# Attention's TensorE order written out by hand: key tiles in pairs, kinds of matmuls grouped, the compressed branch a block ahead, fill tiles emitted last

## The chip, the cores and the metric

The kernel runs on one core of a Trainium2 chip. The metric is the device time of one execution in microseconds (us), the median over runs. TensorE multiplies matrices, VectorE, ScalarE and GpSimd (the profile's DVE, ACT and POOL) do the elementwise work, SyncE (SP) issues most of the DMAs. Each engine works off its own instructions in a fixed order and waits on semaphores for the others.

## The reference, cut to what matters

One block of a network for 1024 tokens of width 1024. A projection `x @ w_in` feeds three branches: `_nsa` (attention, A), `_spatial_gating` (B) and `_mlstm` (C). The outputs of the branches are gated, merged, projected, gated once more and normalized. What the change touches is branch A and the projections that share TensorE with it. Branch A has two groups of four heads; in each, a query sees compressed keys, selected blocks of keys and a window:

```python
p_cmp = _masked_softmax(s_cmp, d_cmp >= 0)                    # 63 compressed keys
o_cmp = einsum(p_cmp, v_cmp)
imp = einsum(p_cmp, overlap)                                  # importance of 16 blocks of 64 keys
top_score, top_idx = lax.top_k(score, 8)                      # 8 blocks for each query
...
o_sel = softmax(q k_sel - slopes * d, causal) v_sel           # the selected blocks
o_w   = softmax(q k_w - slopes * d, window of 256) v_w        # the window
o = gates[0] * o_cmp + gates[1] * o_sel + gates[2] * o_win
y_a = o * silu(a_z)                                           # a_z = x @ w
y_b = u * mixed * silu(b_z)                                   # u = gelu(b_u); b_u, b_z = x @ w
```

## The kernel before, in words

The kernel is written with Tile: the program is emitted in Python, and a planner orders each engine's instructions by priority (what is emitted earlier goes first, what is ready earlier may overtake), hands out the buffers of the pools and sets the semaphores. Each projection multiplies in three parts (high x high, low x high, high x low) to keep float32's accuracy, with operands split into `hi` and `lo`.

- `load_w` (lines 84 to 95) loads a weight tile of 128x1024 into `wraw`, casts it to `whi` on ScalarE (line 92) and subtracts for `wlo` on VectorE (line 93). Each of the three tags has two buffers, and every weight tile of attention and of the next stage goes through them.
- `proj_half` (line 129) makes one half of a projected tile: 24 matmuls of 512 columns into one bank of `pj`. A tile is two halves, 48 matmuls.
- `prep_group(g)` projects a group's k (one tile, lines 372 to 382) and q (two tiles, lines 390 to 403) into `KA`, `KB`, `QA`, `QB`.
- `attn_front(g, qb, d)` handles a block of 128 queries: the compressed branch (scores `ps_c` at line 427, softmax, for qb >= 4 the ranking of the blocks, transposes `ps_t`, `ps_co` at line 472, output `o`), the mask of the selected blocks (`ps_r` and line 464, into `QB[64:80]`), and then the row maxima of the window (`ps_w`) and the selected branch (`ps_s`), eight or twelve matmuls, each reduced by VectorE in `rowmax` (lines 409 and 412). The maxima are transposed (`ps_m`) and written into `QB[96:104]` at line 499.
- `attn_back(g, qb, d, st)` takes the key tiles of a block one after the other: two score matmuls into a bank of `ps_st` (lines 513, 514), the exponential on ScalarE into `pt` (line 516), on some tiles a mask on GpSimd, and four matmuls with the values into `ps_o` (line 536; eight instructions in the trace). The scores run one tile ahead (`AHEAD = 1`). At the end of the window and of the selected branch VectorE adds into `o` (lines 543 to 547), and `o` is transposed (`ps_ot`, line 551) into `ya`.
- `fill_az`, `fill_bu`, `fill_bz` project tiles of `a_z`, `b_u`, `b_z`, which nothing in attention waits for. Seven tiles are emitted in group 0's loop and five in group 1's, half a tile for each block and the rest behind the loop, so group 0's are emitted ahead of `prep_group(1)`.

For a group the loop emits `prep_group`, then for each block the front, half a fill tile and the back of the block before. The order on TensorE is the planner's. Behind attention follow `wtm` projections in 256 columns (line 150), the small work of branch B and the gates of branch C, and from 587 us Strassen products (line 792).

Of the kernel before, what the change touches and what calls it, by code (L numbers as in the profile page):

```python
# [26 lines left out]
WARM = 8  # L27
AHEAD = 1
WB = 2
# [16 lines left out]
def hybrid_kernel(ctx, tc, xm, pT, wfm, wvg, wtm, cmpw1, cmpw2, cpos, vecs, sgwT, sgb,  # L46
# [129 lines left out]

    def silu2(dst, src, n):

        t = tp.tile([P, 512], F32, tag="ge_a", bufs=2, name="si_a")
        act(t[:, :n], src, AF.Tanh, scale=0.5)  # L180
        stt(out=dst, in0=t[:, :n], scalar=1.0, in1=src, op0=OP.add, op1=OP.mult)
# [232 lines left out]

    def attn_front(g, qb, d):
        QA = d["QA"][qb // 2][:, qb % 2]
        QB = d["QB"][qb // 2][:, qb % 2]
        st = {}

        cb = pa2.tile([P, 4, 64], F32, tag="cb", bufs=1, name="cb")  # L420
# [18 lines left out]
        if qb >= 4:  # L439
# [19 lines left out]
            vv.tensor_scalar(out=rk, in0=rk, scalar1=7.5, scalar2=NEG, op0=OP.is_ge, op1=OP.mult)  # L459
            if "rk" in dbg:  # L460
                dump("rk", rk) if (g, qb) == (0, 5) else None
            pr = pst("m", 2, "ps_r")
            nc.tensor.transpose(pr[0:16, 0:P], rk, ident)
            vv.tensor_copy(QB[64:80, :, :], pr[0:16, 0:P].unsqueeze(1).to_broadcast([16, 4, P]))
        ptp = pst("m", 2, "ps_t")
        for a in range(2):
            nc.tensor.transpose(ptp[:, a * P:a * P + P], p[:, 2 * a:2 * a + 2, :], ident)
        pts = pa2.tile([P, 2, P], F32, tag="pts", bufs=2, name="pts")
        nc.any.tensor_copy(out=pts, in_=ptp[:, 0:256].rearrange("p (a q) -> p a q", a=2))
        pco = pst("m", 2, "ps_co")  # L470
        for a in range(2):
# [3 lines left out]
                      gates[:, qb, g * 4:g * 4 + 4].unsqueeze(2).to_broadcast([P, 4, 64]))  # L475
        st["o"] = o

        mx = pa2.tile([P, 8], F32, tag="mx", bufs=3, name="mx")
        mx2 = pa2.tile([P, 4], F32, tag="mx2", bufs=3, name="mx2")
        j0 = max(0, qb - 2)  # L480
        nw = (qb - j0 + 1) * P
        for h in range(HPG):
            pw = pst("m", 2, "ps_w")
            mm(pw[:, 0:nw], lhsT=QB[:, h, :], rhs=d["KBw"][:, j0 * P:j0 * P + nw], start=True, stop=True)
            rowmax(mx[:, 4 + h:5 + h], pw, nw, winm[:, 384 - nw:384] if qb >= 2 else zrow[:, 512 - nw:512])
        ns = (qb + 1) * P
        for h in range(HPG):
            for c0 in range(0, ns, 512):
                n = min(512, ns - c0)
                last = c0 + n == ns  # L490
# [3 lines left out]
                rowmax(dst[:, h:h + 1], pw, n, zrow[:, 512 - n:512] if last else None)  # L494
        if ns > 512:
# [4 lines left out]
                         in1=nblk.unsqueeze(2).to_broadcast([8, 4, P]), op=OP.mult)  # L500
        return st

    def attn_back(g, qb, d, st):
        QA = d["QA"][qb // 2][:, qb % 2].rearrange("p h q -> p (h q)")
        QB = d["QB"][qb // 2][:, qb % 2].rearrange("p h q -> p (h q)")
        o = st["o"]
        sc = pa2.tile([P, 16], F32, tag="osc", bufs=3, name="osc")
        tiles = [("w", j) for j in ([qb - 1, qb, qb - 2] if qb > 1 else range(qb + 1))] + [("s", j) for j in range(qb + 1)]

        def scores(br, j):  # L510
            sp = pst("st", 2, "ps_st")
            ks = slice(j * P, j * P + P)
            mm(sp, lhsT=d["KA" + br][:, ks], rhs=QA, start=True, stop=False)  # L513
            mm(sp, lhsT=d["KB" + br][:, ks], rhs=QB, start=False, stop=True)  # L514
            pt = pa2.tile([P, 4, P], F32, tag="pt", bufs=3, name="pt")
            act(pt.rearrange("p h q -> p (h q)"), sp, AF.Exp)  # L516
            if j == qb:
                nc.gpsimd.affine_select(out=pt, in_=pt, pattern=[[0, 4], [1, P]], compare_op=OP.is_ge,  # L518
                                        fill=0.0, base=0, channel_multiplier=-1)
            elif br == "w" and j == qb - 2:  # L520
                nc.gpsimd.affine_select(out=pt, in_=pt, pattern=[[0, 4], [-1, P]], compare_op=OP.is_gt,
                                        fill=0.0, base=0, channel_multiplier=1)
            return pt

        ahead = [scores(*t) for t in tiles[:AHEAD]]
        for i, (br, j) in enumerate(tiles):
            if i + AHEAD < len(tiles):
                ahead.append(scores(*tiles[i + AHEAD]))
            pt = ahead[i]
            first = i == 0 or tiles[i - 1][0] != br  # L530
            last = i == len(tiles) - 1 or tiles[i + 1][0] != br
            if first:
                po = pst("o", 2, "ps_o")
            vi = g if br == "s" else 2 + g
            for h in range(HPG):
                mm(po[:, h * 65:h * 65 + 65], lhsT=pt[:, h, :], rhs=V[:, j, vi, :],  # L536
                   start=(first and h == 0), stop=last, skip_group_check=True)
            if not last:
                continue
            po3 = po[:, 0:260].rearrange("p (h d) -> p h d", h=4)  # L540
            c0 = 0 if br == "w" else 8
            gi = (16 if br == "w" else 8) + g * 4
            vv.tensor_scalar_max(sc[:, c0:c0 + 4].unsqueeze(2), po3[:, :, 64:65], 1e-30)
            vv.reciprocal(sc[:, c0 + 4:c0 + 8], sc[:, c0:c0 + 4])
            vv.tensor_mul(sc[:, c0 + 4:c0 + 8], sc[:, c0 + 4:c0 + 8], gates[:, qb, gi:gi + 4])
            for h in range(HPG):
                stt(out=o[:, h, :], in0=po3[:, h, 0:64], scalar=sc[:, c0 + 4 + h:c0 + 5 + h], in1=o[:, h, :],
                    op0=OP.mult, op1=OP.add)
        pt2 = pst("o", 2, "ps_ot")
        for a in range(2):  # L550
            nc.tensor.transpose(pt2[:, a * P:a * P + P], o[:, 2 * a:2 * a + 2, :], ident)
        for a in range(2):
            y = ya[2 * g + a][:, qb * P:qb * P + P]
            if g == 0:
                nc.any.tensor_copy(out=y, in_=pt2[:, a * P:a * P + P])
            else:
                stt(out=y, in0=pt2[:, a * P:a * P + P], scalar=0.5, in1=y, op0=OP.mult, op1=OP.mult)

    yb = [yp.tile([P, T], F32, tag="y", bufs=YB, name="yb") for _ in range(4)]

    def fill_az(i):
        w = wf(FM["az"] + i)
        for half in range(2):
            po = pj()
            proj_half(po, w, half, xh, xl)
            y = ya[i][:, half * 512:half * 512 + 512]
            if i >= 2:
                silu2(y, po, 512)
            else:
                z = pa2.tile([P, 512], F32, tag="zz", bufs=1, name="zz")  # L570
                silu2(z, po, 512)
                stt(out=y, in0=z, scalar=0.5, in1=y, op0=OP.mult, op1=OP.mult)
            yield

    def fill_bu(i):
        w = wf(FM["bu"] + i)
        for half in range(2):
            po = pj()
            proj_half(po, w, half, xh, xl)
            gelu2(yb[i][:, half * 512:half * 512 + 512], po, 512)  # L580
            yield

    def fill_bz(i):
        w = wf(FM["bz"] + i)
        for half in range(2):
            po = pj()
            proj_half(po, w, half, xh, xl)
            z = pa2.tile([P, 512], F32, tag="zz", bufs=1, name="zz")
            silu2(z, po, 512)
            y = yb[i][:, half * 512:half * 512 + 512]  # L590
            vv.tensor_mul(y, y, z)
            yield

    for g in range(G):
        fills = chain(*([fill_az(2), fill_az(3), fill_bu(0), fill_bz(0), fill_bu(1), fill_bz(1), fill_bu(2)] if g == 0 else
                        [fill_az(0), fill_az(1), fill_bz(2), fill_bu(3), fill_bz(3)]))
        d = prep_group(g)
        prev = None
        for qb in range(NT):
            st = attn_front(g, qb, d)  # L600
            next(fills, None)
            if prev is not None:
                attn_back(g, prev[0], d, prev[1])
            prev = (qb, st)
        attn_back(g, prev[0], d, prev[1])
        for _ in fills:
            pass
    if "ya" in dbg:
# [637 lines left out]
```

## Time and profile before

| | us |
|---|---|
| median of 3 runs | 1365.41 (1363.35 to 1366.42) |
| the profiled execution | 1363.39 |
| its span, first to last instruction | 1361.6 |
| TensorE busy (PE) | 1334.0 |
| VectorE busy (DVE) | 849.0 |
| ScalarE busy (ACT) | 522.3 |

The times that the rows carry are counted from the span's start. Attention of group 0 runs from about 99 to 277 us, that of group 1 from about 323 to 495. A float32 matmul appears as two instructions of TensorE. Matmuls overlap, so that an instruction's own duration (0.39 us for 512 columns) is longer than the spacing of two (0.23); in the chain of work an instruction counts only until the next one starts. PEclk is the clock granted to TensorE as a share of 2.4 GHz.

### The profile page before, as it was taken

The numbers are of one execution on the slowest core, as the hardware profiler recorded it, in microseconds if no ns is written. First come the engines' busy times: TensorE is split into PE (matmuls) and PEld (weight loads), VectorE is DVE, ScalarE is ACT, GpSimd is POOL, SyncE is SP. The second block draws the span as 40 slices with busy tenths as digits, with TensorE's granted clock in tenths as the row PEclk, the third lists the DMA queues.
The fourth block names the chain that finished last, engine by engine and source line by source line (L and its number), as shares of the span: only waits on it lengthen the run. The fifth ranks groups of instructions, "written<-read, shape, count | busy, mean of one in ns | idle before, by whom it ended". The sixth has DMA issues, their size and how long they took to land.

```text
span 1361.6 us, 18953 instructions
## 1 busy us (share of the span) xinstructions
PE 1334.0 (98%) x7135; PEld 1127.7 (83%) x7135; DVE 849.0 (62%) x2006; ACT 522.3 (38%) x1040; POOL 158.4 (12%) x173
## 2 busy tenths in 40 slices
PE   8999999999999999999999999999999999999997
PEld 6977888887888998988888888888878887888786
DVE  6246777435777748657777678766444555334855
ACT  6353434344333343245455454554442212224211
POOL 0011212101221100001001010010000443000312
PEclk9999999999999999999999999999999999999998
DMA  9131011011110033433222232245346643114201
GB/s 318 32 71 47 24 28 47 19 52 55 55 55 20 17 110 93 141 93 124 97 83 99 94 124 93 62 135 190 117 166 212 201 140 108 47 62 136 96 32 47
DMA packets 48059, 127.46 MB, mean 94 GB/s; under 512 B 5208, under 2 KB 16344, under 8 KB 47968
## 3 DMA queue, kind: packets, MB, share of 16 engines
q1 hardware_dynamic: 47008, 123.11, 27.6%
q0 software_dynamic: 960, 3.15, 1.1%
q8 instruction: 56, 0.92, 0.3%
q14 instruction: 35, 0.29, 0.1%
HBM read 101.00 MB, written 25.23 MB: 93 GB/s over the span
## 4 chain that ended last, share of the span: by engine, by line
PE 85%; DVE 7%; DMA 3%; ACT 3%; issue 2%; POOL 0%; SPq 0%; ACTq 0%; DVEq 0%; POOLq 0%
PE ps_pj L129 19%; PE ps_a L792 13%; PE ps_b L129 9%; PE ps_b L792 7%; PE ps_o L536 7%; PE ps_g L1061 5%; PE ps_c L792 3%; PE ps_st L513 2%; PE ps_pj L150 2%; PE ps_v L138 2%; PE ps_st L514 2%; PE ps_e L1101 2%; PE ps_st L150 1%; PE ps_s L492 1%; DMA xraw<-in_xm_dram 1%
## 5 line engine op out<-in xcount | busy, mean ns | idle before, releaser
L536 PEld LDWEIGHTS ps_o<-V,pt 128*128 128x128 f32 x912 | 117.5, 191 | 12.2 <-ACT pt L516 3.3
L129 PE MATMUL ps_pj<-xh,whi 128*128 128x512 f32 x288 | 115.4, 401 | 2.4 <-DVE QA L402 2.4
L536 PE MATMUL ps_o<-V,pt 128*128 128x65 f32 x912 | 116.7, 269 | 0.5 <-POOL pt L518 0.3
L129 PE MATMUL ps_pj<-xh,wlo 128*128 128x512 f32 x288 | 114.6, 398 | 0.0
L129 PE MATMUL ps_pj<-xl,whi 128*128 128x512 f32 x288 | 114.3, 397 | 0.0
L516 ACT ACTIVATE pt<-ps_st 128x512 f32<-128x512 f32 x114 | 65.4, 594 | 103.7 <-PE ps_st L514 96.6
L792 PE MATMUL ps_a<-op_lo,sh 128*128 128x512 f32 x240 | 94.1, 392 | 0.0
L792 PE MATMUL ps_a<-op_hi,sh 128*128 128x512 f32 x240 | 93.8, 391 | 0.0
L792 PE MATMUL ps_a<-op_hi,sl 128*128 128x512 f32 x240 | 93.8, 391 | 0.0
L779 DVE TENSOR_TENSOR sl<-ss,sh 128x512 fp32r<-128x512 f32 x80 | 54.8, 688 | 59.1 <-ACT sh L778 58.9
L92 ACT CAST whi<-wraw 128x1024 fp32r<-128x1024 f32 x46 | 48.2, 1048 | 77.0 <-PE ps_b L129 46.8
L129 PE MATMUL ps_b<-sp_hi,wlo 128*128 128x512 f32 x192 | 74.8, 390 | 1.3 <-DVE wlo L93 1.3
L129 PE MATMUL ps_b<-sp_lo,whi 128*128 128x512 f32 x192 | 74.7, 389 | 0.0
L129 PE MATMUL ps_b<-sp_hi,whi 128*128 128x512 f32 x192 | 73.9, 389 | 0.0
L93 DVE TENSOR_TENSOR wlo<-wraw,whi 128x1024 fp32r<-128x1024 f32 x46 | 61.5, 1337 | 13.5 <-ACT whi L92 9.3
L1020 POOL TENSOR_TENSOR M<-M,gt 128x512 f32<-128x512 f32 x32 | 42.8, 1350 | 200.0 <-DVE gt L1019 184.4
L129 PEld LDWEIGHTS ps_pj<-xh,whi 128*128 128x128 f32 x288 | 54.2, 188 | 13.6 <-PE ps_pj L129 4.0
L129 PEld LDWEIGHTS ps_pj<-xl,whi 128*128 128x128 f32 x288 | 54.2, 188 | 9.8
L129 PEld LDWEIGHTS ps_pj<-xh,wlo 128*128 128x128 f32 x288 | 54.2, 188 | 8.8
L778 ACT CAST sh<-mraw 128x512 fp32r<-128x512 f32 x60 | 37.3, 622 | 57.1 <-PE ps_a L792 30.8
L778 ACT CAST sh<-ss 128x512 fp32r<-128x512 f32 x80 | 49.6, 620 | 23.0 <-PE ps_b L792 22.2
L779 DVE TENSOR_TENSOR sl<-mraw,sh 128x512 fp32r<-128x512 f32 x60 | 42.9, 716 | 22.8 <-ACT sh L778 22.8
(370 smaller groups left out, 3536.5 us busy)
## 6 DMA issues: line engine op xcount, KB each, us to landing
mraw<-in_wfm_dram SPq DMA_DIRECT2D x40, 512.0 KB, 3.7
gsc<-gt SPq DMA_DIRECT2D x24, 512.0 KB, 2.6
gt<-gsc SPq DMA_DIRECT2D x24, 512.0 KB, 3.8
wraw<-in_wfm_dram SPq DMA_DIRECT2D x18, 512.0 KB, 3.6
xraw<-in_xm_dram SPq DMA_DIRECT2D x14, 512.0 KB, 6.1
yraw<-ysc SPq DMA_DIRECT2D x12, 512.0 KB, 4.4
wraw<-in_wbr_dram SPq DMA_DIRECT2D x12, 512.0 KB, 4.6
wraw<-in_wtm_dram SPq DMA_DIRECT2D x8, 512.0 KB, 3.7
```

The source lines that it names most:

```text
L92: nc.scalar.copy(hi[:, c], raw[:, c])
L93: vv.tensor_sub(lo[:, c], raw[:, c], hi[:, c])
L129: mm(po[:M, :], lhsT=a[:, k, :], rhs=b(k, half), start=(i == 0), stop=(i == n - 1))
L138: mm(po[:, :n], lhsT=tok(a, k, tt), rhs=b[:, k % 4, :], start=(i == 0), stop=(i == tot - 1))
L150: mm(po, lhsT=tok(a, 4 * i + k, tt), rhs=b[:, k, :], start=(i == 0 and tt % 2 == 0 and k == 0 and j == 0), stop=(i == 1 and k == 3 and j = ...
L516: act(pt.rearrange("p h q -> p (h q)"), sp, AF.Exp)
L536: mm(po[:, h * 65:h * 65 + 65], lhsT=pt[:, h, :], rhs=V[:, j, vi, :], start=(first and h == 0), stop=last, skip_group_check=True)
L778: nc.scalar.copy(hi, src)
L779: vv.tensor_sub(lo, src, hi)
L792: mm(bank, lhsT=l[a][:, k, :], rhs=r[b], start=first and k == 0 and i == 0, stop=k == K - 1 and i == 2, skip_group_check=True)
L1020: nc.gpsimd.tensor_add(M[n][:, s], M[n][:, s], t[:, s])
L1061: mm(po[:, 0:n], lhsT=a[k][:, ts_], rhs=b[k][:, s], start=(k == 0 and i == 0), stop=(k == KT - 1 and i == 2))
```

## The change

The loop of blocks is put into a region in which TensorE's instructions keep the order in which they are emitted; the other engines' order, and where TensorE instructions that are emitted outside of the region fall between, stay the planner's. `attn_front` becomes two generators, `attn_cmp` (the compressed branch, in three parts) and `attn_max` (the row maxima, one matmul at a time); `attn_back` becomes the class `Back`, which takes the key tiles in pairs: four score matmuls, and one pair later the values of both tiles. `pt` has four buffers instead of three. The compressed branch of a block is started one step ahead. The fill tiles are emitted behind both groups, `b_u` and `b_z` first and all four of `a_z` last; `a_z` now multiplies into `ya` for all four tiles, so that `finish` copies for both groups. `zz` takes a buffer of `ge_a`, in a pool that outlives attention. The computed result is the same.

```diff
-    def attn_front(g, qb, d):
+    def attn_cmp(g, qb, d):
...
+        yield
         ptp = pst("m", 2, "ps_t")
...
+        if qb >= 4:
+            pr = pst("m", 2, "ps_r")
+            nc.tensor.transpose(pr[0:16, 0:P], rk, ident)
+            vv.tensor_copy(QB[64:80, :, :], pr[0:16, 0:P].unsqueeze(1).to_broadcast([16, 4, P]))
+        yield
         pco = pst("m", 2, "ps_co")
...
+        d["o", qb] = o
+        yield
+
+    def attn_max(g, qb, d):
...
+            yield
...
-        ahead = [scores(*t) for t in tiles[:AHEAD]]
...
+    class Back:
...
+            self.n = (len(self.tiles) + 1) // 2
...
+        def group(self, k):
+            return range(2 * k, min(2 * k + 2, len(self.tiles)))
+
+        def scores(self, k):
+            qb, d = self.qb, self.d
+            for i in self.group(k):
...
+                pt = pa2.tile([P, 4, P], F32, tag="pt", bufs=4, name="pt")
...
+        def values(self, k):
...
+            for i in self.group(k):
...
+        def finish(self):
+            pt2 = pst("o", 2, "ps_ot")
+            for a in range(2):
+                nc.tensor.transpose(pt2[:, a * P:a * P + P], self.d["o", self.qb][:, 2 * a:2 * a + 2, :], ident)
+            for a in range(2):
+                y = ya[2 * self.g + a][:, self.qb * P:self.qb * P + P]
                 nc.any.tensor_copy(out=y, in_=pt2[:, a * P:a * P + P])
-            else:
-                stt(out=y, in0=pt2[:, a * P:a * P + P], scalar=0.5, in1=y, op0=OP.mult, op1=OP.mult)
...
-    for g in range(G):
-        fills = chain(*([fill_az(2), fill_az(3), fill_bu(0), fill_bz(0), fill_bu(1), fill_bz(1), fill_bu(2)] if g == 0 else
-                        [fill_az(0), fill_az(1), fill_bz(2), fill_bu(3), fill_bz(3)]))
-        d = prep_group(g)
-        prev = None
-        for qb in range(NT):
-            st = attn_front(g, qb, d)
-            next(fills, None)
-            if prev is not None:
-                attn_back(g, prev[0], d, prev[1])
-            prev = (qb, st)
-        attn_back(g, prev[0], d, prev[1])
-        for _ in fills:
-            pass
+    with tc.manual_schedule(engines={mybir.EngineType.PE}):
+        for g in range(G):
+            d = prep_group(g)
+            cmp_ = attn_cmp(g, 0, d)
+            next(cmp_)
+            next(cmp_)
+            for step in range(NT + 1):
+                back = Back(g, step - 1, d) if step else None
+                mxs = attn_max(g, step, d) if step < NT else iter(())
+                nmx = (4 + HPG * (1 + step // 4)) if step < NT else 0
+                last = back.n if back else 2
+                done = 0
+                for k in range(last + 1):
+                    upto = nmx * (k + 1) // (last + 1)
+                    mid = (done + upto + 1) // 2
+                    for _ in range(done, mid):
+                        next(mxs)
+                    if back and k < back.n:
+                        back.scores(k)
+                    for _ in range(mid, upto):
+                        next(mxs)
+                    done = upto
+                    if k == 0:
+                        if step < NT:
+                            next(cmp_)
+                        cmp_ = attn_cmp(g, step + 1, d) if step + 1 < NT else iter(())
+                        next(cmp_, None)
+                    if back and k:
+                        back.values(k - 1)
+                if back:
+                    back.finish()
+                next(mxs, None)
+                next(cmp_, None)
+    for i in range(4):
+        fill_bu(i)
+        fill_bz(i)
+    for i in range(4):
+        fill_az(i)
```

## Rows read from the trace of the kernel before

**Rows 1.** The page, part 1: busy time, share of the span, instructions, by engine.

```profile
PE 1334.0 (98%) x7135; PEld 1127.7 (83%) x7135; DVE 849.0 (62%) x2006; ACT 522.3 (38%) x1040; POOL 158.4 (12%) x173
```

**Rows 2.** Busy us (instructions) of PE, PEld, DVE, ACT, POOL by stretch; PEclk, DMA.

```profile
108.00:277.00 169.00, 168.05 (x1023) 144.16 (x1023) 114.93 (x399) 60.71 (x150) 31.67 (x44) 1.00 0.12 33
277.00:330.00 53.00, 51.68 (x232) 41.38 (x231) 22.33 (x52) 25.26 (x60) 2.92 (x4) 1.00 0.16 48
330.00:495.00 165.00, 164.15 (x1054) 143.53 (x1052) 116.84 (x390) 56.27 (x137) 29.36 (x39) 1.00 0.11 36
525.00:550.00 25.00, 22.21 (x176) 20.97 (x175) 22.21 (x75) 5.84 (x11) 0.00 (x0) 1.00 0.10 24
```

**Rows 3.** The same for line 129 alone, group 0: PE, PEld; PEclk, DMA.

```profile
108.00:277.00 169.00, 80.17 (x276) 48.82 (x276) 1.00 0.12 33
```

**Rows 4.** The chain of work: start us, us until the next piece, what.

```profile
239.29 0.84 PE ps_o L536 x8
240.13 0.28 PE ps_st L513
...
259.99 1.73 PE ps_o L536 x16
261.72 0.28 PE ps_st L513
262.00 0.23 PE ps_st L514
...
272.58 3.47 PE ps_pj L129 x15
```

**Rows 5.** Timeline of loads (L91) and casts (L92): start us, us, engine, line.

```profile
40.32 1.56 SPq L91 DMA_DIRECT2D wraw<-in_wfm_dram  x2
...
207.75 0.33 SPq L91 DMA_DIRECT2D wraw<-in_wfm_dram  x1
...
76.68 1.05 ACT L92 CAST whi<-wraw 128x1024 fp32r<-128x1024 f32 x1
...
99.22 1.06 ACT L92 CAST whi<-wraw 128x1024 fp32r<-128x1024 f32 x1
...
272.04 1.04 ACT L92 CAST whi<-wraw 128x1024 fp32r<-128x1024 f32 x1
```

**Rows 6.** Groups by line, DVE, group 0: busy us, mean ns | idle before.

```profile
L93 DVE TENSOR_TENSOR wlo<-wraw,whi 128x1024 fp32r<-128x1024 f32 x6 | 7.3, 1219 | 0.5 <-ACT whi L92 0.5
L173 DVE SCALAR_TENSOR_TENSOR ge_a<-ge_a,ps_pj 128x512 f32<-128x512 f32 x4 | 2.7, 684 | 1.2 <-ACT ge_a L172 1.2
```

**Rows 7.** Timeline at the end of group 0's last block.

```profile
271.58 1.00 PE L536 MATMUL ps_o<-V,pt 128*128 128x65 f32 x8
...
272.78 0.15 DVE L543 TENSOR_SCALAR osc<-ps_o 128x4 f32<-128x4 f32 x1
...
273.50 0.17 DVE L544 RECIPROCAL osc<-osc 128x4 f32<-128x4 f32 x1
...
274.70 0.15 DVE L545 TENSOR_TENSOR osc<-osc,gates 128x4 f32<-128x4 f32 x1
274.89 0.86 DVE L547 SCALAR_TENSOR_TENSOR o<-ps_o,osc,o 128x64 f32<-128x64 f32 x4
...
275.89 0.27 PE L551 MATMUL ps_ot<-ident,o 128*128 128x128 f32 x1
```

**Rows 8.** Groups by line, DVE, 105 to 300 us.

```profile
L499 DVE TENSOR_TENSOR QB<-ps_m,nblk 8x512 fp32r<-8x512 f32 x8 | 5.5, 683 | 1.8 <-PE ps_m L498 1.6
...
L464 DVE CAST QB<-ps_r 16x512 fp32r<-16x512 f32 x4 | 2.7, 682 | 5.4 <-PE ps_r L463 5.4
```

**Rows 9.** Timeline of the second block's compressed branch, first and last piece.

```profile
111.75 0.61 PE L427 MATMUL ps_c<-kbd,q 128*128 128x128 f32 x4
...
117.01 0.42 DVE L469 COPY pts<-ps_t 128x256 f32<-128x256 f32 x1
```

**Rows 10.** Busy time by stretch, the end of the span.

```profile
1354.00:1362.00 8.00, 0.00 (x0) 0.00 (x0) 4.07 (x10) 0.89 (x1) 1.50 (x1) 0.50 0.17 66
```

More of the change, by code (lines that the diff above doesn't have):

```diff
@@ L2 @@
 from contextlib import ExitStack
-from itertools import chain
 import numpy as np
@@ L27 @@
 WARM = 8
-AHEAD = 1
 WB = 2
@@ L175, in gelu2, with silu2 @@
         stt(out=dst, in0=sq, scalar=1.0, in1=src, op0=OP.add, op1=OP.mult)
-    def silu2(dst, src, n):
-        t = tp.tile([P, 512], F32, tag="ge_a", bufs=2, name="si_a")
+    def silu2(dst, src, n, t=None):
+        if t is None:
+            t = tp.tile([P, 512], F32, tag="ge_a", bufs=2, name="si_a")
         act(t[:, :n], src, AF.Tanh, scale=0.5)
@@ L459, in attn_front @@
             vv.tensor_scalar(out=rk, in0=rk, scalar1=7.5, scalar2=NEG, op0=OP.is_ge, op1=OP.mult)
[L460 to L464, printed above, removed]
+        yield
         ptp = pst("m", 2, "ps_t")
@@ L475, in attn_front @@
                       gates[:, qb, g * 4:g * 4 + 4].unsqueeze(2).to_broadcast([P, 4, 64]))
-        st["o"] = o
+        d["o", qb] = o
+        yield
+    def attn_max(g, qb, d):
+        QB = d["QB"][qb // 2][:, qb % 2]
         mx = pa2.tile([P, 8], F32, tag="mx", bufs=3, name="mx")
@@ L489, in attn_front @@
                 n = min(512, ns - c0)
-                last = c0 + n == ns
                 pw = pst("m", 2, "ps_s")
@@ L493, in attn_front @@
                 dst = mx if c0 == 0 else mx2
-                rowmax(dst[:, h:h + 1], pw, n, zrow[:, 512 - n:512] if last else None)
+                rowmax(dst[:, h:h + 1], pw, n, zrow[:, 512 - n:512] if c0 + n == ns else None)
+                yield
         if ns > 512:
@@ L500, in attn_front @@
                          in1=nblk.unsqueeze(2).to_broadcast([8, 4, P]), op=OP.mult)
[L501 to L523, printed above, removed]
-        ahead = [scores(*t) for t in tiles[:AHEAD]]
[L526 to L554, printed above, removed]
@@ new lines, in attn_tiles, with __init__ @@
+    def attn_tiles(qb):
+        return [("w", j) for j in ([qb - 1, qb, qb - 2] if qb > 1 else range(qb + 1))] + [("s", j) for j in range(qb + 1)]
+    class Back:
+        def __init__(self, g, qb, d):
+            self.g, self.qb, self.d = g, qb, d
+            self.tiles = attn_tiles(qb)
+            self.n = (len(self.tiles) + 1) // 2
+            self.pts = {}
+            self.QA = d["QA"][qb // 2][:, qb % 2].rearrange("p h q -> p (h q)")
+            self.QB = d["QB"][qb // 2][:, qb % 2].rearrange("p h q -> p (h q)")
+        def group(self, k):
[3 more added lines that the diff above has]
+            for i in self.group(k):
+                br, j = self.tiles[i]
+                sp = pst("st", 2, "ps_st")
+                ks = slice(j * P, j * P + P)
+                mm(sp, lhsT=d["KA" + br][:, ks], rhs=self.QA, start=True, stop=False)
+                mm(sp, lhsT=d["KB" + br][:, ks], rhs=self.QB, start=False, stop=True)
+                pt = pa2.tile([P, 4, P], F32, tag="pt", bufs=4, name="pt")
+                act(pt.rearrange("p h q -> p (h q)"), sp, AF.Exp)
+                if j == qb:
+                    nc.gpsimd.affine_select(out=pt, in_=pt, pattern=[[0, 4], [1, P]], compare_op=OP.is_ge,
+                                            fill=0.0, base=0, channel_multiplier=-1)
+                elif br == "w" and j == qb - 2:
+                    nc.gpsimd.affine_select(out=pt, in_=pt, pattern=[[0, 4], [-1, P]], compare_op=OP.is_gt,
+                                            fill=0.0, base=0, channel_multiplier=1)
+                self.pts[i] = pt
+        def values(self, k):
+            g, qb = self.g, self.qb
+            tiles = self.tiles
+            if k == 0:
+                self.sc = pa2.tile([P, 16], F32, tag="osc", bufs=3, name="osc")
+            o, sc = self.d["o", qb], self.sc
+            for i in self.group(k):
+                br, j = tiles[i]
+                pt = self.pts.pop(i)
+                first = i == 0 or tiles[i - 1][0] != br
+                last = i == len(tiles) - 1 or tiles[i + 1][0] != br
+                if first:
+                    self.po = pst("o", 2, "ps_o")
+                po = self.po
+                vi = g if br == "s" else 2 + g
+                for h in range(HPG):
+                    mm(po[:, h * 65:h * 65 + 65], lhsT=pt[:, h, :], rhs=V[:, j, vi, :],
+                       start=(first and h == 0), stop=last, skip_group_check=True)
+                if not last:
+                    continue
+                po3 = po[:, 0:260].rearrange("p (h d) -> p h d", h=4)
+                c0 = 0 if br == "w" else 8
+                gi = (16 if br == "w" else 8) + g * 4
+                vv.tensor_scalar_max(sc[:, c0:c0 + 4].unsqueeze(2), po3[:, :, 64:65], 1e-30)
+                vv.reciprocal(sc[:, c0 + 4:c0 + 8], sc[:, c0:c0 + 4])
+                vv.tensor_mul(sc[:, c0 + 4:c0 + 8], sc[:, c0 + 4:c0 + 8], gates[:, qb, gi:gi + 4])
+                for h in range(HPG):
+                    stt(out=o[:, h, :], in0=po3[:, h, 0:64], scalar=sc[:, c0 + 4 + h:c0 + 5 + h], in1=o[:, h, :],
+                        op0=OP.mult, op1=OP.add)
+        def finish(self):
[4 more added lines that the diff above has]
+                y = ya[2 * self.g + a][:, self.qb * P:self.qb * P + P]
@@ L566, in fill_az @@
             y = ya[i][:, half * 512:half * 512 + 512]
[L567 to L573, printed above, removed]
+            z = tp.tile([P, 512], F32, tag="ge_a", bufs=2, name="zz")
+            act(z, po, AF.Tanh, scale=0.5)
+            stt(out=z, in0=z, scalar=1.0, in1=po, op0=OP.add, op1=OP.mult)
+            stt(out=y, in0=z, scalar=0.5, in1=y, op0=OP.mult, op1=OP.mult)
     def fill_bu(i):
@@ L580, in fill_bu @@
             gelu2(yb[i][:, half * 512:half * 512 + 512], po, 512)
-            yield
     def fill_bz(i):
@@ L587, in fill_bz @@
             proj_half(po, w, half, xh, xl)
-            z = pa2.tile([P, 512], F32, tag="zz", bufs=1, name="zz")
-            silu2(z, po, 512)
+            z = tp.tile([P, 512], F32, tag="ge_a", bufs=2, name="zz")
+            silu2(z, po, 512, z)
             y = yb[i][:, half * 512:half * 512 + 512]
             vv.tensor_mul(y, y, z)
-            yield
-    for g in range(G):
-        fills = chain(*([fill_az(2), fill_az(3), fill_bu(0), fill_bz(0), fill_bu(1), fill_bz(1), fill_bu(2)] if g == 0 else
-                        [fill_az(0), fill_az(1), fill_bz(2), fill_bu(3), fill_bz(3)]))
-        d = prep_group(g)
-        prev = None
-        for qb in range(NT):
-            st = attn_front(g, qb, d)
-            next(fills, None)
-            if prev is not None:
-                attn_back(g, prev[0], d, prev[1])
-            prev = (qb, st)
-        attn_back(g, prev[0], d, prev[1])
-        for _ in fills:
-            pass
+    with tc.manual_schedule(engines={mybir.EngineType.PE}):
[20 more added lines that the diff above has]
+                    done = upto
+                    if k == 0:
+                        if step < NT:
[8 more added lines that the diff above has]
+                next(cmp_, None)
```

1 line of the change is left out of this document (removed).

## The prediction

> **What bounds the kernel now.** I read the page's first part, then the busy time by stretch, then the chain of work, then single stretches of the timeline. TensorE is busy for 98% of the span [rows 1]. By stretch it stays so through attention: 168.05 of 169 us in group 0, 164.15 of 165 in group 1, 51.68 of 53 between them, at a granted clock of 1.00 (the 2.4 GHz level) [rows 2]. TensorE's instruction stream is thus the bound, and the reader is to see how little can be won: the idle time of these three stretches is 0.95 + 1.32 + 0.85 = 3.1 us. VectorE is not far behind: 114.93 us of those 169 [rows 2]. What fills TensorE's waits in group 0 is the projection work of the fill tiles: 276 of the 1023 matmuls are those of line 129 [rows 3], one each 3.47/15 = 0.23 us [rows 4], 276 x 0.23 = 63.8 us. Without them group 0 has 169 - 63.8 = 105.2 us of TensorE work, and VectorE, less the fills' own part, 114.9 - 7.3 (L93, six) - 12.9 (five groups of 512 wide operations like the one shown, 19 in all, at 0.68) = 94.7 us [rows 2, 6]. Two engines this close, tied by chains, can't both be kept full by one fixed order. That is the ground on which I price the change.
>
> **Grouping the kinds of matmul.** Today a key tile is 2 score matmuls and 8 instructions of the values: 0.28 + 0.23 + 0.84 = 1.35 us. The score matmul behind the values takes 0.28 instead of 0.23, and this looks like a price of changing kinds. But 16 value instructions in a row take 1.73, not 2 x 0.84 = 1.68: what the first score matmul loses, the last value instruction had won. A pair is 1.73 + 0.28 + 3 x 0.23 = 2.70 us, two single tiles are 2 x 1.35 = 2.70 [rows 4]. So 114 tiles in pairs gain nothing; the bound to either side is 57 x 0.05 = 2.9 us.
>
> **TensorE's order fixed.** The region fixes the order of TensorE's instructions alone. An instruction that waits now holds up everything of attention behind it. Only work emitted outside the region, the fill tiles, can be put in its place. So all turns on whether fill tiles are ready in group 0. Their projections need three buffers that they share with the q and k weights of `prep_group`: `wraw`, `whi`, `wlo`, two of each. The loads go ahead as soon as a buffer is free, in the order of emission. The two loads of line 91 from 40.32 fetch the third and fourth tile, while the third is cast only at 76.68 and the fifth at 99.22. The load at 207.75 is the k tile of group 1, though its cast, the eleventh in order, runs at 272.04, 64 us later [rows 5]. In the changed text the fourth, fifth and sixth tiles are no fills but group 1's k, q, q, because `prep_group(1)` is now emitted ahead of every fill. A tile is 48 matmuls, 48 x 0.23 = 11 us; so by the same eagerness group 1's k is cast at about 77 + 11 = 88 us and its first q at about 99 us. They then hold both `whi` and both `wlo` until group 1's projections run, and these stand behind all of group 0 in TensorE's fixed order. **No fill can have its weights before that.** Group 0's attention runs without filler, and the 63.8 us of fill work return at the end.
>
> The idle time that this leaves in group 0, step by step:
> (a) Ends of steps. `finish` transposes o right behind the last values. The chain is: values end at 272.58, L543 0.2 later (0.15), L544 0.17, L545 0.15, four L547 in 0.86, the transpose 0.14 after them, in sum 1.7 us [rows 7]. (The row pieces are added without the other work that VectorE did between them.) Then the maxima are transposed and line 499 writes them into QB: 0.68 [rows 8] plus 0.3 of hand-over, 1.0. Where the next block has a mask of selected blocks, line 464 adds 0.68 [rows 8], and the next max matmul waits for it. Of nine steps, step 0 pays 1.0; steps 1, 2 and 7 pay 2.7 less 0.2 for a max matmul under it; steps 3 to 6 pay 1.7 + 1.0 + 0.7 less 0.1; step 8 pays 1.7. Sum 1.0 + 7.5 + 13.2 + 1.7 = 23.4 us.
> (b) The start. From the compressed scores to their copied transposes runs 111.75 to 117.43 [rows 9], 5.7 us, of which TensorE works 0.6. Ahead of step 0 nothing stands under it (5.1); in step 0, for block 1, some 1.5 us of small matmuls do, and 1.0 is counted above (3.2). For steps 1 and 2, with 2 and 4 tiles (2.7 and 5.4 us) against 8 maxima and a softmax on VectorE, I estimate 2. Sum 10.
> (c) Steps 3 to 7 have VectorE and TensorE about even, with two `m` banks between them: 1 us a step by my estimate, 0 to 2.5. Sum 5.
> Together 38.4 us. Of such waits the 105.2 already holds some 4 by estimate: 0.95 in the open [rows 2], the rest as spacing between matmuls. Net **+34 us**.
>
> Group 1 has its fills: both buffers come free as its q tiles are projected, 133 us of fill work (12 tiles of 48 matmuls) stand ready and some 35 us of waits want them. There, and between the groups, I expect 1.3 us won of the 1.32 idle [rows 2]. Behind attention the fills run dense, and the `zz` buffer has left attention's pool, so the next stage's small work can start under them: of the 2.8 us idle in 525 to 550 [rows 2] I take half, 1.4. The other edits I cost at nothing. The az tiles' four more 0.68 us operations, the copy in place of the product for group 1 and the fourth `pt` buffer all lie beside a busy TensorE. The stores of `ya` move behind the last fill, and with them the `xraw` loads, on SP; the projections of four 256 column blocks that no longer run under attention cover them. If that cover failed, about 4 us. Net of these gains: 34 - 2.7 = +31.
>
> **Sum.** The profiled execution took 1363.39 us (span 1361.6 and 1.8 around it); 1363.4 + 31 = 1394.4. It lies 2.0 below the median of the three runs, 1365.41, so on the scale of the median **1396 us**.
>
> One page speaks about emitting the filler apart: the Trainium skill, "Perfetto Trace Analysis", section Optimization Strategy, says that a kernel whose busiest engine changes may gain when its regimes are interleaved. The trace agrees so far as group 0's 169 us, with fills in it, leave TensorE 0.95 idle [rows 2]; by that rule taking them out costs what I summed from the rows, with no price of its own.
>
> **Rivals.**
> 1. Fills get the buffers in time (the planner gives them `whi` ahead of group 1's tiles, or loads group 1 late). Then every wait of the hand order is covered in both groups; the place is 87 to 99 us, and it decides whether the fourth and fifth cast are fills. Speaking against: the loads' strict order of emission [rows 5]. The price is the rest of today's idle: 3.1 + 2.8 = 5.9 us at most [rows 2], 0 at least: 1359.5 to 1365.4, I take **1360**. This is the side of not slower. Chance 0.15.
> 2. Blocked, but cheap: of (a) to (c) only the ends of steps are paid, and half of those lie under max matmuls: 23.4/2 - 2.7 = +9, up to +15: **1376**. For it: VectorE's work is below TensorE's. Chance 0.05.
> 3. Blocked, and the granted clock falls in the gaps. The rows show it low at the end: in 1354 to 1362, where TensorE runs no matmul any more, it is 0.50, the 1.2 GHz level [rows 10]. Against it: 2.8 us of idle within 525 to 550 cost no clock [rows 2]. At the lower level work takes double; if a quarter of the 105 us fell there, +26: **1422**. Chance 0.05. The Trainium skill, "TensorE: Matmul & The Clock Gate", section Why this matters for your kernels, says to keep TensorE continuously busy or see it go back to the low rate; the end of the trace agrees, and the first wait of (b) is where it would show.
> 4. The change does not do what it says: the planner's order was the same already. Rows 4 exclude it: tiles run there one by one at 239 us and two at once at 260 us.
>
> **How the numbers follow.** My forecast has 0.75. Its own range runs from (a) alone, 23.4 - 4 - 2.7 = +17 (1382), to (c) at its upper end and a short fall of the clock, +52 (1418). With rival 1's upper part and rival 2, the range 1361 to 1418 leaves about 2 in 10 out (most of rival 1 and all of rival 3). About 0.2% is what a measurement of this kernel can tell from no change: 1362.7 to 1368.1. Faster 0.13 (rival 1 but for its slow end), same 0.05, slower 0.82.
>
> **What would show it.** Right: casts of line 92 at about 87 and 99 us with no projection of line 129 between some 100 us and the end of group 0; group 0 ending near 250 us with TensorE busy for 75 to 80%; gaps ahead of `ps_ot` of 1.5 to 2 us, eight times; a dense run of line 129 behind group 1. Wrong: fills between group 0's matmuls, TensorE at 98% there (rival 1); gaps below 1 us (rival 2); a clock below 1.00 in group 0 (rival 3); pairs that take clearly less than 2.70 us (the grouping pays).

## The result, and the profile after

The changed kernel takes **1433.13 us** (1430.52 to 1434.98), 1.0496 times the time before [1.0472, 1.052], some 68 us more. The forecast was 1396 us in a range of 1361 to 1418: the sign was right, the size too small by 37 us, and the measured time lies above the range. The profiled execution after took 1434.98 us, 1.9 above its median, and that of before lies 2.0 below its own, so differences of the two traces come out about 4 us larger than those of the medians.

The page of the changed kernel, part 1 (engine, busy us) and of part 2 the lines of TensorE and its clock (40 slices of 36 us):

```profile
PE 1370.2 (96%) x7135; PEld 1157.1 (81%) x7135; DVE 843.8 (59%) x1988; ACT 529.1 (37%) x1062; POOL 152.1 (11%) x173
...
PE   9977878998999999999999999999999999999997
...
PEclk9995779899999999999999999999999999999999
```

Against [rows 1] TensorE is busy 36.2 us longer with the same 7135 instructions: not only waits were added, the instructions became slower. The clock line says where, in slices 4 to 8, which is group 0.

Busy time by stretch in the kernel before (columns as in [rows 2]), up to the first Strassen product and behind it:

```profile
0.00:587.20 587.20, 575.39 (x3591) 502.61 (x3591) 368.30 (x1103) 228.03 (x514) 70.53 (x102) 1.00 0.23 70
98.00:277.00 179.00, 177.49 (x1068) 151.30 (x1067) 120.40 (x411) 67.10 (x169) 33.14 (x46) 1.00 0.12 35
...
587.20:1362.00 774.80, 758.64 (x3544) 625.05 (x3544) 480.72 (x904) 294.25 (x527) 87.88 (x71) 0.99 0.34 111
```

The same in the changed kernel, with group 0, the projections between, group 1 and the rest up to the first Strassen product by themselves:

```profile
0.00:659.30 659.30, 611.65 (x3592) 532.06 (x3592) 363.20 (x1085) 234.99 (x536) 64.04 (x102) 0.93 0.21 62
98.00:274.00 176.00, 141.06 (x760) 120.57 (x760) 98.78 (x379) 54.21 (x152) 29.93 (x46) 0.76 0.07 19
274.00:314.00 40.00, 38.86 (x173) 31.52 (x171) 13.83 (x26) 20.94 (x52) 2.94 (x4) 1.00 0.15 43
314.00:474.70 160.70, 156.12 (x959) 133.47 (x960) 109.93 (x393) 58.61 (x153) 26.07 (x39) 0.98 0.08 23
474.70:659.30 184.60, 181.28 (x1186) 166.61 (x1184) 96.70 (x200) 51.87 (x75) 0.11 (x1) 0.99 0.32 99
659.30:1434.00 774.70, 758.54 (x3544) 625.07 (x3544) 480.61 (x904) 294.08 (x527) 88.11 (x71) 0.99 0.34 111
```

Behind the first Strassen product nothing changed (774.8 and 774.7 us). Ahead of it 72.1 us were lost, and these rows split them: TensorE's idle time (length less busy) rose from 11.8 to 47.7 us, **+35.8**, and its busy time for the same instructions from 575.4 to 611.7, **+36.3**. Nearly all lies in group 0: 34.9 us idle, and a busy time that at the old pace would be 177.5 less the 308 matmuls that left it, 308 x 0.23 = 70.8, so 106.7 instead of 141.1: +34.4. The granted clock of 0.76 accounts for some 30 of these: a mean of 0.76 of levels 1.00 and 0.50 is 0.48 x 176 = 84 us at 0.50, TensorE is busy there for some 72% (rows below), 61 us, of which half would have done.

Line 127 alone (129 before; PE and PEld, clock, DMA), in group 0, group 1 and behind it, which answers [rows 3]:

```profile
108.00:274.00 166.00, 0.23 (x1) 0.31 (x2) 0.76 0.06 16
...
314.00:474.70 160.70, 57.74 (x206) 35.99 (x206) 0.98 0.08 23
474.70:560.00 85.30, 78.75 (x347) 64.88 (x346) 0.99 0.26 81
```

One projection matmul in group 0, where there were 276, and a dense run of 347 behind group 1. The timeline of loads (line 89) and casts (line 90) says why, and answers [rows 5]:

```profile
78.81 11.04 SPq L89 DMA_DIRECT2D wraw<-in_wfm_dram  x2
...
101.42 0.33 SPq L89 DMA_DIRECT2D wraw<-in_wfm_dram  x1
...
288.25 11.04 SPq L89 DMA_DIRECT2D wraw<-in_wfm_dram  x2
...
87.19 1.05 ACT L90 CAST whi<-wraw 128x1024 fp32r<-128x1024 f32 x1
99.05 1.04 ACT L90 CAST whi<-wraw 128x1024 fp32r<-128x1024 f32 x1
```

The fourth and fifth tile are cast at 87.19 and 99.05, then no weight is cast and, after 101.42, none loaded until 288.25, when group 1's projections free the buffers.

TensorE's longest waits in group 0 (98 to 274 us; us, times, longest):

```profile
PE ps_ot L574 <- DVE o L568: 13.8, 8, 3.3
PE ps_t L461 <- DVE pcm L436: 8.7, 2, 7.1
PE ps_s L495 <- DVE mx L411: 2.8, 5, 1.8
PE ps_w L487 <- DVE QB L467: 2.3, 3, 0.8
```

The end of a step in the changed kernel, block 4 (timeline: start us, us, engine, line):

```profile
202.68 2.42 PE L557 MATMUL ps_o<-V,pt 128*128 128x65 f32 x16
...
205.14 0.16 DVE L564 TENSOR_SCALAR osc<-ps_o 128x4 f32<-128x4 f32 x1 [1.52 <-PE ps_o L557]
...
205.75 0.86 DVE L568 SCALAR_TENSOR_TENSOR o<-ps_o,osc,o 128x64 f32<-128x64 f32 x4
...
206.37 0.77 PE L574 MATMUL ps_ot<-ident,o 128*128 128x128 f32 x2 [1.27 <-DVE o L568]
...
207.39 0.68 DVE L503 TENSOR_TENSOR QB<-ps_m,nblk 8x512 fp32r<-8x512 f32 x1 [0.78 <-PE ps_m L502]
...
208.66 0.68 DVE L467 CAST QB<-ps_r 16x512 fp32r<-16x512 f32 x1 [0.59 <-PE ps_r L466]
...
209.40 0.69 PE L487 MATMUL ps_w<-KBw,QB 128*128 128x384 f32 x1 [0.77 <-DVE QB L467]
```

The values end, VectorE works at the denominators and `o` while TensorE stands 1.27 us ahead of `ps_ot`, then 0.77 ahead of the next maximum. That is the chain of [rows 7, 8], in the open.

Now the clock, by stretch in the changed kernel:

```profile
100.00:110.00 10.00, 3.46 (x14) 3.12 (x15) 5.07 (x17) 4.08 (x16) 0.95 (x2) 0.57 0.24 66
110.00:120.00 10.00, 7.23 (x23) 5.27 (x23) 5.32 (x25) 3.00 (x11) 2.08 (x4) 0.50 0.05 13
...
180.00:190.00 10.00, 7.10 (x24) 5.64 (x25) 4.93 (x21) 2.10 (x5) 0.03 (x1) 0.50 0.00 0
...
340.00:470.00 130.00, 129.93 (x822) 113.12 (x820) 88.34 (x305) 47.98 (x121) 18.91 (x29) 1.00 0.06 17
```

and the same 16 value instructions in the chain of work, within such a stretch and outside of one:

```profile
122.84 3.32 PE ps_o L557 x16
137.10 1.73 PE ps_o L557 x16
```

In the first wait of 7.1 us the granted clock falls to 0.50, the 1.2 GHz level, and it falls there again at the ends of most steps; 16 instructions then take 3.32 us instead of the 1.73 that they take outside and in [rows 4]. In group 1, with fills, TensorE is busy for 129.93 of 130 us at 1.00.

### The profile page after: what moved, and what is told of

Same layout as the page of the kernel before. It is cut to its first block, busy times and chain, and to the rows that moved or that the text cites. A ratio compares the mean times of both kernels' runs of the same rounds, so it can differ in the third digit from the quotient of the medians.

```text
span 1433.0 us, 18930 instructions
## 1 busy us (share of the span) xinstructions
PE 1370.2 (96%) x7135; PEld 1157.1 (81%) x7135; DVE 843.8 (59%) x1988; ACT 529.1 (37%) x1062; POOL 152.1 (11%) x173
## 4 chain that ended last, share of the span: by engine, by line
PE 85%; DVE 7%; DMA 3%; ACT 3%; issue 1%; POOL 0%; SPq 0%; DVEq 0%; ACTq 0%; POOLq 0%
PE ps_pj L127 17%; PE ps_a L833 13%; PE ps_b L127 9%; PE ps_b L833 7%; PE ps_o L557 6%; PE ps_g L1102 5%; PE ps_st L148 3%; PE ps_pj L148 3%; PE ps_c L833 3%; PE ps_st L529 2%; PE ps_st L530 2%; PE ps_v L136 2%; PE ps_e L1142 1%; PE ps_s L495 1%; PE ps_w L487 1%
## 5 line engine op out<-in xcount | busy, mean ns | idle before, releaser
L557 PE MATMUL ps_o<-V,pt 128*128 128x65 f32 x912 | 113.1, 279 | 0.0
L91 DVE TENSOR_TENSOR wlo<-wraw,whi 128x1024 fp32r<-128x1024 f32 x46 | 61.2, 1330 | 25.9 <-ACT whi L90 21.8
L127 PEld LDWEIGHTS ps_pj<-xh,wlo 128*128 128x128 f32 x288 | 54.2, 188 | 10.3
L819 ACT CAST sh<-ss 128x512 fp32r<-128x512 f32 x80 | 49.6, 620 | 22.9 <-PE ps_b L833 22.1
```

Of the source, the lines that this page charges most:

```text
L91: vv.tensor_sub(lo[:, c], raw[:, c], hi[:, c])
L127: mm(po[:M, :], lhsT=a[:, k, :], rhs=b(k, half), start=(i == 0), stop=(i == n - 1))
L819: nc.scalar.copy(hi, src)
```

## The experiments

All are read in one way: when the first Strassen product starts, how long TensorE was idle until then, and how long busy. From the busy time that of the added filler matmuls is taken, at 0.23 us each; what remains above 575.4 is matmuls slowed by the clock (the order moves it too, by some us: a matmul behind a wait shows its whole length).

| kernel | us | first Strassen product | idle | busy less filler |
|---|---|---|---|---|
| before | 1365.4 | 587.2 | 11.8 | 575.4 |
| changed | 1433.1 | 659.3 | 47.7 | 611.7 |
| e1_dummies | 1423.6 | 647.1 | 13.7 | 633.4 - 55.2 = 578.2 |
| e2_two_regions | 1371.3 | 596.0 | 14.9 | 581.1 |
| e3_planner_fills_last | 1454.7 | 683.0 | 34.1 | 648.9 |
| e4_two_regions_single | 1374.6 | 597.4 | 13.7 | 583.7 |
| e5_cover_by_hand | 1419.8 | 643.7 | 27.5 | 616.2 - 23.7 = 592.5 |
| e6_dummies_120 | 1425.9 | 648.6 | 28.5 | 620.1 - 27.6 = 592.5 |
| e7_late_finish | 1361.5 | 586.1 | 9.7 | 576.5 |
| e8_fills_last_late | 1414.9 | 640.2 | 40.6 | 599.6 |
| e9_single_two_ahead | 1362.1 | 584.2 | 9.0 | 575.2 |

The theory: fills that can't come into group 0 leave waits there, and the waits pull the clock down. The rivals: the hand order itself is slow, or VectorE's chains set the pace whatever the clock.

**e2_two_regions: give the fills back.** A region for each group, the eight `b` fills emitted between them:

```diff
-    with tc.manual_schedule(engines={mybir.EngineType.PE}):
-        for g in range(G):
+    for g in range(G):
+        with tc.manual_schedule(engines={mybir.EngineType.PE}):
...
-    for i in range(4):
-        fill_bu(i)
-        fill_bz(i)
+        if g == 0:
+            for i in range(4):
+                fill_bu(i)
+                fill_bz(i)
```

> The changed kernel with a region for each group and the eight b_u and b_z tiles emitted between the two, ahead of prep_group(1); the hand order is unchanged. Theory (fills blocked by buffers that group 1's tiles take first): fills stand in both groups, the clock stays at 1.00, total 1358 to 1368. Rival (the hand order itself costs, fills or not): 1400 or more.

Measured 1371.29 us, ratio 1.0051 [1.0039, 1.0064]. Line 127 alone, in group 0 and from there to the end of group 1:

```profile
108.00:268.00 160.00, 57.13 (x205) 36.02 (x205) 0.98 0.11 30
268.00:503.00 235.00, 120.14 (x488) 89.12 (x487) 1.00 0.13 41
```

205 projection matmuls are back in group 0, and 62 of the 68 us with them: the place of emission is the cause. Some 7 us (0.5%) stay, 3 more than the expected range (1358 to 1368) allowed, and the clock in group 0 is 0.98 and not 1.00.

**e3_planner_fills_last: the late fills alone.** The kernel before with the planner's order of attention; only the fills are emitted behind both groups, with the copy, the `a_z` product and the `zz` buffer as in the change:

```diff
-            next(fills, None)
...
-        for _ in fills:
+    for i in range(4):
+        for f in (fill_bu(i), fill_bz(i)):
+            for _ in f:
+                pass
+    for i in range(4):
+        for _ in fill_az(i):
             pass
```

> The kernel before with its own order by the planner (single tiles, one ahead) but with the fill tiles emitted behind both groups. Theory (the place of emission is the cause): no projection in group 0's attention, clock below 1.00 there, total 1400 to 1435. Rival (the hand order is the cause): about 1365.

Measured 1454.72 us (1449.14 to 1459.61), ratio 1.0661 [1.0629, 1.0693], above the expectation and slower than the changed kernel. Group 0 and 20 us of it, by stretch, and two of its waits (us, times, longest), the one that is the longest in total and the one with the longest single wait:

```profile
98.00:307.40 209.40, 186.47 (x815) 150.87 (x814) 107.94 (x386) 58.63 (x159) 29.83 (x46) 0.70 0.07 18
...
220.00:240.00 20.00, 19.81 (x89) 17.68 (x88) 8.65 (x31) 4.55 (x8) 2.45 (x4) 0.60 0.05 14
...
PE ps_s L493 <- DVE mx L413: 4.3, 15, 0.6
...
PE ps_pj L129 <- DVE KAw L383: 1.4, 1, 1.4
```

So the late fills alone cost more than the whole change; the rival "the hand order is slow" falls. The planner's order waits less in group 0 (22.9 us against 34.9), but its clock is 0.70 over the group. From 120 to 300 us no projection matmul runs there.

**e1_dummies: fill the waits with work that nobody reads.** The changed kernel and 240 matmuls into one bank, emitted behind the region, placed by the planner. The bank is one of the two of `pj`; it is taken and written once ahead of attention, so that it need not wait behind group 1's projections, which use `pj` too. By the text of the program the fills are thus blocked twice, by the weight buffers and by the banks; no run separates the two.

```diff
+            if g == 0:
+                idle = pj()
+                mm(idle, lhsT=tok(xh, 0, 0), rhs=xh(0, 0), start=True, stop=True, skip_group_check=True)
...
+    for r in range(240):
+        mm(idle, lhsT=tok(xh, r % 8, r % 4), rhs=xh(r % 8, 0), start=True, stop=True, skip_group_check=True)
```

> The changed kernel with 240 matmuls (512 columns, x with x, into one bank that nobody reads; 240 x 0.23 = 55 us) emitted behind the region. They need no weights, so the planner can put them into group 0's waits; the fill tiles stay where they are. Theory (buffers block the fills; the waits cost some 35 us and the low clock some 36 us on top): granted clock about 1.00 in group 0, the group's attention about 140 us long instead of 173, total 1395 to 1405. Rival (the clock is a symptom, the waits are all): clock up, but group 0 still about 170 us, total 1430 or more.

Measured 1423.61 us, ratio 1.0435 [1.0421, 1.0449]. Group 0 by stretch:

```profile
98.70:259.90 161.20, 160.02 (x992) 137.31 (x991) 98.83 (x379) 52.80 (x152) 29.89 (x46) 1.00 0.08 21
```

The total lies between the theory's 1395 to 1405 and the rival's 1430: both missed. The clock is back at 1.00 and the idle time gone, but group 0 takes 161 us, not 140. Of the 240 filler matmuls 234 stand in it (53.8 us), so its 161.2 us are 1.2 idle, 53.8 filler and 106.2 of attention's own work. I had put some 55 us of filler into some 35 us of waits and not counted that the rest delays attention. But the 161 could also be the pace of VectorE's chains, so two more runs.

**e5_cover_by_hand and e6_dummies_120: less filler.** e5 writes 103 such matmuls into group 0's fixed order at the waits; e6 is e1 with 120 instead of 240.

```diff
+            if g == 0:
+                idle = pj()
+            def cover(n):
+                for r in range(n if g == 0 else 0):
+                    mm(idle, lhsT=tok(xh, r % 8, r % 4), rhs=xh(r % 8, 0), start=True, stop=True, skip_group_check=True)
+            cover(24)
             next(cmp_)
+            cover(2)
...
+                        cover(4 if step == 0 else 0)
...
+                    cover(8 if step in (1, 3) else 5)
                     back.finish()
                 next(mxs, None)
+                cover(3)
```

> The changed kernel with 103 filler matmuls written into group 0's fixed order, just where its waits are: 26 at the start, 4 in step 0, 5 or 8 ahead of each finish, 3 behind each transpose of the maxima; 23.7 us of matmuls that nobody reads. They delay nothing that is ready, only the waits are shorter. Theory A (waits of some 35 us and the granted clock at 0.50 beside them, some 36 us): the clock stays near 1.00, the waits with their cover stay 35 us, group 0's attention takes 105 + 35 = 140 us and ends at about 240 us instead of 273.7, in all 1393 to 1408 us. Theory B (the clock cost little of its own: at full clock the same chains on VectorE set the pace, as the 161 us of e1_dummies may say): group 0 ends at 255 to 262 us, in all 1413 to 1423.

> e1_dummies with 120 filler matmuls instead of 240 (27.6 us instead of 55.2), placed by the planner. Theory A (in e1_dummies 55 us of filler stood in 35 us of waits and held attention up by some 20): group 0 ends some 15 to 20 us earlier than e1_dummies' 259.9, in all 1400 to 1410 us. Theory B (VectorE's chains set the 161 us, the filler only stood beside): group 0 ends within 5 us of 259.9, in all 1415 to 1425.

Measured: e5 1419.81 us, ratio 1.04 [1.0386, 1.0413]; e6 1425.86, ratio 1.0444 [1.043, 1.0457], slower than with 240. Group 0 and its first stretch at the low clock in e5, and group 0 in e6:

```profile
98.40:259.70 161.30, 145.95 (x859) 123.50 (x858) 98.86 (x379) 53.50 (x152) 29.87 (x46) 0.93 0.08 20
...
112.00:129.00 17.00, 15.27 (x51) 12.17 (x51) 9.25 (x45) 3.42 (x14) 2.71 (x4) 0.51 0.03 9
...
98.70:265.30 166.60, 150.45 (x878) 128.33 (x876) 99.08 (x379) 53.59 (x152) 29.91 (x46) 0.90 0.08 20
```

Theory A's times were missed in both; e5 falls into B's range, and e6 lies just above it, in time (by 0.9 us) and in the end of group 0 (5.4 us behind that of e1, where B allowed 5). The 161.3 us of e5 are 15.4 idle, 23.0 filler (100 of the 103 stand in this stretch), the 106.2 of e1, and 16.7 more. Idle and filler together are 38.4 where the waits were 34.9, so the cover hit them; but it didn't hold the clock. At 0.93 over the group some 23 us lie at the low level (0.51 in 112 to 129), 90% busy, which by this estimate costs 10 of the 16.7; what the other 7 are is open. Without the clock's part group 0 would take about 150 us, between A's 140 and B's 155 to 162: the two are not told apart in full, and no run reached that point. If B holds in part, its share is at most the 4 us more of waits and those 7. In e6, the smaller filler took 26 us out of group 0, and idle time (16.2 instead of 1.2) and the clock (0.90) gave back more: 166.6 us against 161.2. A filler is worth both the wait that it covers and the clock that it holds.

**e7_late_finish: take the chain out of the step's end.** e2 with `finish` of a block moved behind the first scores of the next step:

```diff
+            late = None
...
                     if k == 0:
+                        if late:
+                            late.finish()
                         if step < NT:
...
-                if back:
+                late = back
+                if step == NT:
                     back.finish()
                 next(mxs, None)
```

> e2_two_regions with finish of a block moved behind the first pair of scores of the next step (the last block's stays). Theory: what e2_two_regions still loses to the kernel before (6 us) is the open wait of 3.25 us ahead of ps_ot at 125.5 us and the half clock around it (6.8 us, so 3.4); both go: 1363 to 1368 us. Rival: the loss is the hand order's small waits all over, or the wait turns up at the write of the maxima: 1369 to 1373.

Measured **1361.52 us** (1360.5 to 1363.72), ratio 0.9975 [0.9964, 0.9986]: 9.8 us below e2 and a little faster than the kernel before (0.25%). Up to the first Strassen product, and the one stretch where the clock still falls:

```profile
0.00:586.10 586.10, 576.45 (x3592) 506.82 (x3592) 359.41 (x1086) 233.06 (x535) 64.20 (x102) 0.99 0.23 70
...
120.00:129.00 9.00, 7.76 (x33) 6.22 (x32) 7.99 (x32) 2.91 (x8) 1.81 (x3) 0.62 0.19 59
```

Idle falls from 14.9 to 9.7 us, busy from 581.1 to 576.5. So the hand order, with fills to stand in its waits, is not slower than the planner's.

**e8_fills_last_late: the same in the changed kernel**, where no fill covers (the edit as in e7).

> The changed kernel (fills last, one region) with the later finish of e7_late_finish. In the changed kernel the waits ahead of ps_ot are 13.8 us of group 0's 35; the late finish takes them. Theory A (these waits also are what pulls the granted clock down in steps 2 to 8, 51 us at 0.50 behind 140 us, some 19 us of the 32): 1433 - 13 - 19 = 1401, between 1395 and 1408, the clock near 1.00 behind 140 us. Theory B (the other waits, 0.5 to 1.8 us each, keep it down as well): 1433 - 13 = 1420, between 1414 and 1424. Theory C (the wait only moves to the transpose of the maxima): 1428 to 1434.

Measured 1414.94 us, ratio 1.0361 [1.0345, 1.0376]; waits in group 0:

```profile
PE ps_t L461 <- DVE pcm L436: 10.6, 3, 7.1
PE ps_w L487 <- DVE QB L467: 4.5, 4, 1.4
...
PE ps_r L466 <- DVE rk L457: 2.1, 1, 2.1
PE ps_ot L574 <- DVE o L568: 1.4, 2, 1.3
```

It falls into B's range, and B is not all of it. The wait ahead of `ps_ot` went from 13.8 to 1.4 us, but the idle time only from 47.7 to 40.6: the rest came up at the next links of the chain (C in part). The busy time fell by 12.1 with it (A in part), but the clock of A, near 1.00 behind 140 us, did not come: it is 0.90 in 140 to 260, against 0.81 in 140 to 274 of the changed kernel.

**e4_two_regions_single and e9_single_two_ahead: is it the grouping?** e4 is e2 with one tile in a group; e9 is e7 with one tile in a group but the scores two ahead, so that little but the alternation of kinds differs from e7 (the row maxima are spread over more turns of the loop, too).

```diff
-            self.n = (len(self.tiles) + 1) // 2
+            self.n = len(self.tiles)
...
-            return range(2 * k, min(2 * k + 2, len(self.tiles)))
+            return range(k, k + 1)
...
-                last = back.n if back else 2
+                last = back.n + 1 if back else 2
...
-                    if back and k:
-                        back.values(k - 1)
+                    if back and k > 1:
+                        back.values(k - 2)
```

(the last two hunks in e9 alone)

> As e2_two_regions, but a group is one key tile instead of two. Theory (grouping the kinds of matmuls is worth nothing: a pair takes 2.70 us, two single tiles take 2.70): the same as e2_two_regions within 3 us. Rival (each change of kind costs 0.05 us or more): slower than e2_two_regions by 3 us or more.

> e7_late_finish with key tiles one by one, the scores two tiles ahead of the values, so that the kinds of matmuls alternate but the exponential has as much time as with pairs. If grouping the kinds is worth nothing by itself, as the prediction has it (2.70 us a pair either way), the same as e7_late_finish within 3 us: 1359 to 1364. If changing kinds costs: 57 pairs with one change more of 0.05 us is 2.9, up to 57 x 0.1 = 5.7 us more: 1364.5 to 1367.5.

Measured: e4 1374.55 us, 3.3 above e2, by the letter on the rival's side of the 3 us; e9 1362.07 (1359.75 to 1363.58), ratio 0.9975 [0.9964, 0.9985], that of e7, and within the theory's range. Pairs help by the longer way from scores to values, if at all; grouping the kinds is worth nothing that can be measured.

## Why the prediction was wrong, point by point

- **The bound and the grouping**: as predicted. TensorE's stream is the bound, attention's own work in group 0 is 106.2 us (e1) against 105.2, and a pair is worth two single tiles (e9).
- **The blocked fills**: right, to the time of the casts (87.19 and 99.05 against 87 to 88 and 99). The `pj` banks, a second block by the text of the program, were not seen.
- **The waits in group 0**: right, in the net partly by luck. 34.9 us idle against 38.4; by terms, (a) some 20 instead of 23.4 (`ps_ot` 13.8, the rest at the writes of QB and the transposes behind them), (b) 8.7 of `ps_t` instead of 10, (c) about 4 of `ps_s` instead of 5. I deducted 4 that 105.2 would already hold, where the trace of before has 1.5 idle; idle rose by 33.4, against +34: the terms were 3.5 too high and the deduction 2.5, and the two errors nearly cancel.
- **The gains elsewhere**: wrong, small. Idle outside of group 0 was to fall by 2.7 and rose from 10.3 to 12.7 us; group 1's first step waits 3.25 us ahead of `ps_ot`, and a wait of 2.1 us at the start of the next stage stayed.
- **The clock: this step failed.** The sum of 1396 us has no term for it: it took TensorE's 105.2 us of work in group 0 at full clock, and the fall of the clock stood as the third rival, with a chance of 0.05. It came, on top of waits that were right: the granted clock was 0.76 over group 0, TensorE's busy time rose by 36.3 us, some 30 of it in group 0 by the clock, and group 0 ended at 274 us instead of some 250. The rival's price, 26 for a quarter of group 0's work at the low level, was near (30 of 105 us is 0.29); its chance was not, and its 1422 us was the better forecast by far. The ground given against it, that 2.8 us idle in 525 to 550 cost no clock [rows 2], was one stretch, 89% busy, most of its idle in one wait of 2.1 us; group 0 without fills is 80% busy with waits at every step. (The busy share alone would not have told: group 0 of e3 is 89% busy too, at a clock of 0.70.) I priced the waits of a stretch and not what the stretch becomes with them. The range too, up to 1418, allowed only a short fall of the clock beside the waits.

The Trainium skill, "TensorE: Matmul & The Clock Gate", section Why this matters for your kernels, advises against long idle gaps between bursts of matmuls, as they bring the low rate back. The wait of 7.1 us at the start of group 0, with a clock of 0.50 behind it, agrees; e3 goes beyond that: no wait in its group 0 is longer than 1.4 us, and its clock is 0.70.

What stays open: whether weight buffers of the fills' own would do without the second region; no run tried it. Nor did any run show attention of group 0 at full clock with its waits bare.

## What to carry to other kernels

Work that is to stand in the waits of a fixed order needs its buffers (and, by the text of this program, its banks) before the order begins, and this planner hands them out in the order of emission: emit the filler between the fixed regions, not behind them. The stretch in which TensorE lost its filler here cost its waits and about as much again in clock, and in e3 more than twice as much: price both. And take the chain that ends a step out of its place (here the transpose of `o`, one set of scores later); with filler there it was worth 9.8 us.

## What the runs showed of the hardware

The granted clock fell with short waits. In e3 no wait of group 0 is longer than 1.4 us, TensorE is busy for 186.5 of 209.4 us, and the clock is 0.70; in 220 to 240 it is busy for 19.81 of 20 us and still at 0.60: once low, it stayed low there through a busy stretch. In four runs idle time and what the clock cost in group 0, estimated as above from clock and busy share, went together: 34.9 us and some 30 in the changed kernel, 16.2 and 15 in e6, 15.4 and 10 in e5, 1.2 and none in e1. e3 is the exception: 22.9 idle, but 0.60 x 209 = 126 us at the low level, at 89% busy a cost of 56. The length of a wait alone doesn't decide. In the stage behind attention both kernels have one wait of 2.1 us; in the changed kernel the clock falls behind it, in the kernel before it stays at 1.00. These are the changed kernel's 10 us around the wait:

```profile
556.00:566.00 10.00, 7.92 (x54) 7.72 (x53) 8.19 (x8) 1.99 (x2) 0.00 (x0) 0.83 0.56 172
```

and those of the kernel before:

```profile
541.00:551.00 10.00, 7.88 (x65) 7.56 (x65) 9.05 (x38) 2.53 (x5) 0.00 (x0) 1.00 0.02 6
```

TensorE is busy for the same 7.9 us in both; what makes the difference, no run here tells.
